# Gate and branch projections of a hybrid decoder layer with tokens instead of features on the output partitions

## The chip, the cores and the metric

The kernel runs on one core of one Trainium2 chip. The metric is the time of one execution on the device in microseconds (us). A profile is one further execution, taken by the hardware profiler; TensorE's rows stand under PE (products) and PEld (loads of the left operand), VectorE is DVE, ScalarE is ACT, GpSimd is POOL, and SP is SyncE, which here only issues DMAs.

## The reference

One layer with 256 tokens, model width 2048 and float32 throughout. The input is normalised and projected by `w_in` (2048 x 12288). Its columns feed three branches of width 1024 (a gMLP, an S5 state-space mixer, stick-breaking attention) and three gates of width 2048. The part that matters:

```python
h = rmsnorm(x, norm1_g[l])
proj = h @ w_in[l]
...
gates = jax.nn.sigmoid(proj[..., o_c:].reshape(bsz, seq, N_BRANCHES, D_MODEL) + b_gate[l])
...
ys = jnp.stack([y_a, y_b, y_c], axis=2)
br = jnp.einsum('blnw,nwd->blnd', ys, w_branch[l])
merged = jnp.sum(gates * br, axis=2)
x = x + merged @ w_out[l]
h2 = rmsnorm(x, norm2_g[l])
x = x + jnp.square(jax.nn.relu(h2 @ w_mlp_in[l])) @ w_mlp_out[l]
```

A row's norm is a factor per token; the kernel projects the input times the norm's weight and multiplies by that factor when it takes the product out of PSUM.

## The kernel before

**Products in three passes.** Every float32 product is done in TensorE's faster float32r type: each operand is split into a high part that is exact in that type and the rest, low. A product is high by high, low by high and high by low, added up in PSUM. A class `Split` holds an activation with features on partitions, high and low.

**Units.** All large weights run past as 536 units of 256 rows by 512 columns (512 KB) in one order (`plan`). For a unit SyncE issues the load (`dma_to`, four buffers, five units ahead), ScalarE copies the high part (L198) and VectorE subtracts it for the low one (the rows `lo<-raw,hi`), three units ahead of the products (`conv_to`). A group is the 4 or 8 units of one block of 512 output columns.

**Two forms.** `run_T` (L254) holds 128 x 128 blocks of the weights and streams the 256 tokens past them: the output has features on partitions and tokens along a row, 24 products of 256 columns for a unit (L265, L266 high weights, L273 low weights). `run_N` (L281) holds 128 x 128 blocks of the activation and streams 512 weight columns: the output has tokens on partitions, 12 products of 512 columns for a unit (L294, L295, L297). Both take a PSUM tile per half of a group, and hand it to the group's function `ev` one unit after its last product. A function `later` puts work off by some units.

**Order of the groups.** The projections of S5, attention and gMLP; then for each of four column blocks d gate 2, branch 2, gate 0, branch 0; the four groups of gate 1; two groups of S5's own gate (glu); the four groups of branch 1; the output projection; the MLP. Before the change, all gates and branches use `run_T`; v, the gMLP's v half, the output projection and the second half of the MLP use `run_N`.

**Gates and branches.** `do_gate` multiplies each half of the product by the token factor, which stands along the row (`rb`), and ScalarE adds the bias, one number per partition from the table `colv`, in the sigmoid (L973, four instructions of 128 x 256 for a group). `do_branch` multiplies the gate by the branch's product and adds it to the merged sum; at branch 1 it splits the sum into `ms` at once, which already has features on partitions, as the output projection wants it.

**Side work.** The small work of S5, attention and gMLP is written as generators. After each unit `pump` runs them as long as VectorE's estimated time allows (2560 ns for a unit), up to their next `yield`; `yield BAR` waits for the next unit. Everything is issued in program order on TensorE, VectorE, ScalarE and SyncE, so each engine works through the units with the side work in between. S5's side work lies in the gate stretch; its small products `py` (L716) read rotated states that VectorE has made.

Of the kernel before, what the change touches and what calls it, by code (L numbers as in the profile page):

```python
# [36 lines left out]
# columns of the per-feature vectors  # L37
C_G1, C_G2, C_BG, C_GM, C_D, C_GLU = 0, 16, 32, 80, 88, 96
NCOLS = 104


class Split:
    """A transposed activation [features, tokens] as hi + lo, both exact in float32r."""
# [21 lines left out]
class Metered:  # L65
    """The vector engine, with the time of what has been issued to it (ns)"""
# [22 lines left out]
def hybrid_trunk(  # L89
# [9 lines left out]
    cols: bass.AP,  # L99
    final_g: bass.AP,  # L100
# [37 lines left out]
    # -------------------------------------------------------- weight stream  # L138
# [64 lines left out]
    # ------------------------------------------------------- side work pump  # L203
    BAR = "bar"
    tasks = []
    credit = [0.0]  # vector engine time left to side work
# [24 lines left out]
    # -------------------------------------------------------- matmul groups  # L231
    slot = [0]
    late = []  # evacuations, emitted one unit after the group's last product
# [20 lines left out]
    def run_T(us, src, evac, lead=3, mid=None, delay=1):  # L254
        """out[512 features, tokens]; evac(b, psum [P, 2, T]) for each 256 features"""
        ps = [ps_mm.tile([P, 2, T], F32, tag="mm", name=f"mm{us[0]}_{b}") for b in range(2)]
        nk = len(us)
        for i, u in enumerate(us):
            hi, lo = begin_unit(u, lead)
            for nb in range(4):  # L260
                po = ps[nb // 2][:, nb % 2, :]
                for k in range(2):
                    kt = 2 * i + k
                    wh = hi[:, k, nb * P:(nb + 1) * P]
                    PE.matmul(po, lhsT=wh, rhs=src.hi(kt), start=kt == 0 and nb % 2 == 0, stop=False)  # L265
                    PE.matmul(po, lhsT=wh, rhs=src.lo(kt), start=False, stop=False)  # L266
                if nb == 1 and mid is not None:
                    mid(i)
            for nb in range(4):
                po = ps[nb // 2][:, nb % 2, :]  # L270
                for k in range(2):
                    kt = 2 * i + k
                    PE.matmul(po, lhsT=lo[:, k, nb * P:(nb + 1) * P], rhs=src.hi(kt), start=False,  # L273
                              stop=kt == 2 * nk - 1 and nb % 2 == 1)
            if i == nk - 1:
                for b in range(2):
                    late.append((slot[0] + delay, lambda b=b: evac(b, ps[b])))
                flush()
            end_unit()

    def run_N(us, src, evac):  # L281
        """out[tokens, 512 columns]; evac(tt, psum [P, 512]) for each 128 tokens"""
        ps = [ps_mm.tile([P, 512], F32, tag="mm", name=f"mm{us[0]}_{tt}") for tt in range(NT)]
        nk = len(us)
        for i, u in enumerate(us):
            hi, lo = begin_unit(u, 3)
            for part in range(2):
                for tt in range(NT):
                    for k in range(2):
                        kt = 2 * i + k  # L290
                        xh = src.hi(kt)[:, tt * P:(tt + 1) * P]
                        xl = src.lo(kt)[:, tt * P:(tt + 1) * P]
                        if part == 0:
                            PE.matmul(ps[tt], lhsT=xh, rhs=hi[:, k, :], start=kt == 0, stop=False)  # L294
                            PE.matmul(ps[tt], lhsT=xl, rhs=hi[:, k, :], start=False, stop=False)  # L295
                        else:
                            PE.matmul(ps[tt], lhsT=xh, rhs=lo[:, k, :], start=False,  # L297
                                      stop=kt == 2 * nk - 1)
            if i == nk - 1:
                for tt in range(NT):  # L300
                    late.append((slot[0] + 1, lambda tt=tt: evac(tt, ps[tt])))
            end_unit()

    def run_last(us, src, evac):
        """out[tokens, 512 columns], the first 128 tokens ahead of the others"""
        w = []
        nk = len(us)
        for tt, c0, c1 in ((0, 0, 512), (1, 0, 256), (1, 256, 512)):
            ps = ps_mm.tile([P, 512], F32, tag="mm", name=f"mml{tt}_{c0}")
            po = ps[:, 0:c1 - c0]  # L310
            for kt in range(2 * nk):
                if kt % 2 == 0 and tt == 0:
                    w.append(begin_unit(us[kt // 2], 7))
                    slot[0] += 1
                hi, lo = (t[:, kt % 2, c0:c1] for t in w[kt // 2])
                xh = src.hi(kt)[:, tt * P:(tt + 1) * P]
                xl = src.lo(kt)[:, tt * P:(tt + 1) * P]
                PE.matmul(po, lhsT=xh, rhs=hi, start=kt == 0, stop=False)
                PE.matmul(po, lhsT=xh, rhs=lo, start=False, stop=False)
                PE.matmul(po, lhsT=xl, rhs=hi, start=False, stop=kt == 2 * nk - 1)  # L320
            evac(tt, c0, c1, po)

    # ------------------------------------------------------------- helpers
    def inv_rms(ss, n, name):
        """ss [P, tiles, parts] partial sums of squares -> [P, tiles] (mean + eps) ** -0.5"""
# [15 lines left out]
    def split2(dst, i, src):  # L341
        """src [P, 2, T]: feature tiles 2 i and 2 i + 1"""
# [4 lines left out]
    def transposes(chunk, half, name):  # L347
        """two feature tiles, each in its own bank"""
# [9 lines left out]
    def split_scaled(pts, dst, kt0, gcol):  # L358
        """transposed feature tiles, times the norm's weight"""
# [7 lines left out]
    # ------------------------------------------------- first loads, constants  # L367
# [30 lines left out]
    # ntri[s', s] = -1 where s' > s  # L398
# [4 lines left out]
    # the tensor engine's clock comes up while the first loads are under way  # L403
    pw = side("pwarm")
    wz = cst([P, P], "wz")
    V.memset(wz, 0.0)
    def warm(n):
        for i in range(n):
            PE.matmul(pw[:, 0:P], lhsT=wz, rhs=wz, start=True, stop=True)
# [3 lines left out]
    # --------------------------------------------------------------- norm 1  # L413
# [36 lines left out]
    # ------------------------------------------------------------------- S5  # L450
    s5x = [a4([P, 4, T], F32, f"s5x{i}") for i in range(2)]  # input, then y, then gelu(y)
# [5 lines left out]
    def s5_split_b():  # L457
        """hi and lo of the input matrices, to DRAM; they come back stacked"""
# [52 lines left out]
    def s5_prep():  # L511
# [25 lines left out]
        # k = (exp(lam dt) - 1) / lam  # L537
# [19 lines left out]
        # e1[j, b] = exp(i phi b), e16[j, a] = exp(16 i phi a); cs ends as exp(128 i phi)  # L557
# [33 lines left out]
    def s5_run():  # L591
# [5 lines left out]
        def stack(ch):  # L597
            """u and b of two 32-row blocks, stacked so that one pass is bh uh + bl uh + bh ul"""
# [29 lines left out]
        def make_ck(h):  # L628
# [10 lines left out]
            # minus the imaginary part  # L639
# [4 lines left out]
        def table_a(ch):  # L644
            """exp(i phi t), t < 128"""
# [23 lines left out]
        def table_b(ch):  # L669
            """t >= 128, the parts that go with the sine"""  # L670
# [17 lines left out]
        def rotate(cs, z, sign):  # L688
            """z *= exp(sign i phi t)"""
# [88 lines left out]
    # ------------------------------------------------------------ attention  # L778
# [3 lines left out]
    def attention(half):  # L782
        scale = 1.0 / math.sqrt(P)
        fl = "p e b t -> p (e b t)"
        for hb in (2 * half, 2 * half + 1):
# [11 lines left out]
            for e in range(2):  # L797
                S.activation(za[:, e].rearrange("p b t -> p (b t)"), pz[e][:, 0:T + P], AF.Copy, scale=scale)
                # keep t > s in the two blocks on the diagonal
# [43 lines left out]
    # ----------------------------------------------------------------- gMLP  # L843
# [11 lines left out]
    def gmlp():  # L855
        ws, bs = gm["ws"], gm["bs"]
        # keep s <= t
# [36 lines left out]
    # ------------------------------------------------------- group handlers  # L894
# [68 lines left out]
    def do_gate(n, d, us):  # L963
        def ev(b, ps):
            if b == 0:
                gate[n, d] = a4([P, 4, T], F32, f"gate{n}_{d}")
            gt = gate[n, d]
            V.tensor_mul(gt[:, 2 * b:2 * b + 2, :], ps, rb)

            def act():  # L970
                for nb in (2 * b, 2 * b + 1):
                    c = C_BG + 16 * n + 4 * d + nb
                    S.activation(gt[:, nb, :], gt[:, nb, :], AF.Sigmoid, bias=colv[:, c:c + 1])  # L973

            later(1 + b, act)

        run_T(us, xs, ev)

    def do_branch(n, d, us):
        if n != 1:  # L980
            drain({2: "att1", 0: "gmlp"}[n])
        def ev(b, ps):
            gt = gate[n, d]
            if n == 2:
                merged[d] = gt
            g = gt[:, 2 * b:2 * b + 2, :]
            m = merged[d][:, 2 * b:2 * b + 2, :]
# [3 lines left out]
            if n == 1:  # L991
                split2(ms, 2 * d + b, m)

        run_T(us, {2: yc, 0: ya, 1: yb}[n], ev)
# [84 lines left out]
    # ------------------------------------------------------------- the trunk  # L1079
# [44 lines left out]
def _tiles(w):  # L1124
    """[K, N] -> [N / 512, K / 256, 128, 2, 512]: one contiguous half megabyte per unit"""
# [8 lines left out]
def _layout(x, norm1_g, w_in, b_gate, gm_norm_g, gm_w_s, gm_b_s, s5_lambda_re, s5_lambda_im, s5_log_dt,  # L1134
# [10 lines left out]
    a["cols"] = np.concatenate([_cols(norm1_g[0]), _cols(norm2_g[0]), _cols(b_gate[0]), _cols(gm_norm_g[0]),  # L1145
                                _cols(s5_d[0]), _cols(s5_b_glu[0])], axis=1)
    a["final_g"] = final_g
# [37 lines left out]
```

## Time and profile before

| | us |
|---|---|
| median of 3 runs | 1581.82 |
| lowest and highest | 1581.37 and 1581.89 |
| profiled execution, span from its first to its last instruction | 1579.1 |
| TensorE busy in it | 1564.4 |
| VectorE busy | 1069.1 |
| ScalarE busy | 763.5 |

The profile gives no time around the span of its execution; the median of the runs stands 2.7 us above it. Products are pipelined, so that a single one's row (283 ns for 256 columns, 389 for 512) is longer than its share of the time: what a unit takes is read from the start of one unit to the start of the next. Idle time of an engine that nothing waits for costs nothing.

### The profile page before, as it was taken

What the parts mean: (1) busy time and instruction counts of PE and PEld (TensorE: products, weight loads), DVE (VectorE), ACT (ScalarE), POOL (GpSimd) and SP (SyncE); (2) the same over time, 40 slices, a digit from 0 to 9 for tenths busy, and PEclk for the clock granted to TensorE, in tenths of its full rate; (3) what the DMA queues carried; (4) which work ended last, traced back from release to release, by engine and by line L of the source; (5) the groups of instructions that cost most, each with busy time, mean ns of one, the idle gap of its engine ahead of it and who ended that gap; (6) DMA issues with size and microseconds to landing.
All of it is one profiled execution on the core that took longest, in us unless ns stands there. A gap on an engine that the chain in (4) does not pass through costs nothing.

```text
span 1579.1 us, 26929 instructions
## 1 busy us (share of the span) xinstructions
PE 1564.4 (99%) x11030; PEld 1467.4 (93%) x11030; DVE 1069.1 (68%) x1402; ACT 763.5 (48%) x954; POOL 71.2 (5%) x126
## 2 busy tenths in 40 slices
PE   9999999999999999999999999999999999999996
PEld 9999989999999999999889998899888998899986
DVE  6895889988989898967655555555545555554554
ACT  6436567545454555464444444444433444344442
POOL 0102121000011000000000000000000000000000
PEclk9999999999999999999999999999999999999998
DMA  7868666666666666555665566656666566666663
GB/s 269 249 202 233 189 196 188 187 182 184 193 194 183 186 200 187 161 175 194 220 214 185 170 193 197 191 179 193 187 191 194 177 187 193 193 174 196 214 190 106
DMA packets 95258, 303.84 MB, mean 192 GB/s; under 512 B 11040, under 2 KB 22816, under 8 KB 95136
## 3 DMA queue, kind: packets, MB, share of 16 engines
q1 hardware_dynamic: 79840, 285.25, 59.6%
q0 software_dynamic: 11904, 10.49, 3.4%
q10 hardware_dynamic: 3392, 6.40, 1.2%
q8 instruction: 86, 1.41, 0.4%
q14 instruction: 36, 0.29, 0.1%
HBM read 295.80 MB, written 6.29 MB: 191 GB/s over the span
## 4 chain that ended last, share of the span: by engine, by line
PE 97%; issue 1%; DVE 1%; DMA 1%; ACT 0%; POOLq 0%; POOL 0%; DVEq 0%; ACTq 0%
PE mm L265 21%; PE mm L266 21%; PE mm L273 21%; PE mm L294 11%; PE mm L295 11%; PE mm L297 11%; PE py L716 1%; PE pb L618 0%; DVE x L83 0%; DMA raw<-in_w_m 0%; PE pyc L834 0%; DVE lo L83 0%; PE pm L878 0%; PE zt L353 0%; PE xt L353 0%
## 5 line engine op out<-in xcount | busy, mean ns | idle before, releaser
L83 DVE TENSOR_TENSOR lo<-raw,hi 128x1024 fp32r<-128x1024 f32 (+1 forms) x537 | 652.9, 1222 | 433.4 <-ACT hi L198 432.8
L198 ACT CAST hi<-raw 128x1024 fp32r<-128x1024 f32 (+1 forms) x537 | 557.8, 1048 | 645.6 <-PE mm L266 357.6
L265 PE MATMUL mm<-xs,hi 128*128 128x256 f32 x1280 | 316.0, 284 | 0.6 <-ACT hi L198 0.5
L266 PE MATMUL mm<-xs,hi 128*128 128x256 f32 x1280 | 314.1, 283 | 0.0
L265 PE MATMUL mm<-xz,hi 128*128 128x256 f32 x1024 | 251.4, 283 | 0.0
L266 PE MATMUL mm<-xz,hi 128*128 128x256 f32 x1024 | 251.3, 283 | 0.0
L265 PEld LDWEIGHTS mm<-xs,hi 128*128 128x128 f32 x1280 | 245.4, 192 | 3.5 <-ACT bu L625 2.1
L266 PEld LDWEIGHTS mm<-xs,hi 128*128 128x128 f32 x1280 | 245.5, 192 | 0.0
L266 PEld LDWEIGHTS mm<-xz,hi 128*128 128x128 f32 x1024 | 196.6, 192 | 0.2
L265 PEld LDWEIGHTS mm<-xz,hi 128*128 128x128 f32 x1024 | 196.6, 192 | 0.2
L295 PE MATMUL mm<-hi,ff 128*128 128x512 f32 x480 | 186.8, 389 | 0.0
L294 PE MATMUL mm<-hi,ff 128*128 128x512 f32 x480 | 186.8, 389 | 0.0
L273 PE MATMUL mm<-xs,lo 128*128 128x256 f32 x1280 | 179.7, 283 | 0.0
L273 PEld LDWEIGHTS mm<-xs,lo 128*128 128x128 f32 x1280 | 165.1, 192 | 0.0
L273 PE MATMUL mm<-xz,lo 128*128 128x256 f32 x1024 | 143.7, 283 | 0.0
L273 PEld LDWEIGHTS mm<-xz,lo 128*128 128x128 f32 x1024 | 132.1, 192 | 0.0
L297 PE MATMUL mm<-lo,ff 128*128 128x512 f32 x480 | 128.3, 389 | 0.0
L297 PEld LDWEIGHTS mm<-lo,ff 128*128 128x128 f32 x480 | 90.1, 188 | 18.7
L295 PEld LDWEIGHTS mm<-hi,ff 128*128 128x128 f32 x480 | 90.1, 188 | 18.6
L294 PEld LDWEIGHTS mm<-hi,ff 128*128 128x128 f32 x480 | 90.1, 188 | 18.6
L83 DVE TENSOR_TENSOR rt<-bu,cs 128x1024 f32<-128x1024 f32 x64 | 76.4, 1219 | 0.2
L294 PE MATMUL mm<-hi,xs 128*128 128x512 f32 x128 | 50.5, 394 | 0.0
(241 smaller groups left out, 1732.9 us busy)
## 6 DMA issues: line engine op xcount, KB each, us to landing
raw<-in_w_m SPq DMA_DIRECT2D x256, 512.0 KB, 4.3
raw<-in_w_in SPq DMA_DIRECT2D x191, 512.0 KB, 4.1
raw<-in_w_br SPq DMA_DIRECT2D x48, 512.0 KB, 4.2
raw<-in_w_out SPq DMA_DIRECT2D x32, 512.0 KB, 4.4
raw<-in_w_glu SPq DMA_DIRECT2D x8, 512.0 KB, 4.2
su<-ud POOLq DMA_DIRECT2D x48, 64.0 KB, 5.1
bs<-bd POOLq DMA_DIRECT2D x48, 64.0 KB, 4.8
x<-in_x ACTq DMA_DIRECT2D x4, 512.0 KB, 5.4
```

The costliest lines, as they stand in the source:

```text
L83: return fn(*a, **kw)
L198: S.copy(hi[:, k, :], raw[:, k, :])
L265: PE.matmul(po, lhsT=wh, rhs=src.hi(kt), start=kt == 0 and nb % 2 == 0, stop=False)
L266: PE.matmul(po, lhsT=wh, rhs=src.lo(kt), start=False, stop=False)
L273: PE.matmul(po, lhsT=lo[:, k, nb * P:(nb + 1) * P], rhs=src.hi(kt), start=False, stop=kt == 2 * nk - 1 and nb % 2 == 1)
L294: PE.matmul(ps[tt], lhsT=xh, rhs=hi[:, k, :], start=kt == 0, stop=False)
L295: PE.matmul(ps[tt], lhsT=xl, rhs=hi[:, k, :], start=False, stop=False)
L297: PE.matmul(ps[tt], lhsT=xh, rhs=lo[:, k, :], start=False, stop=kt == 2 * nk - 1)
L716: PE.matmul(py[h][32 * i:32 * i + 32, :T], lhsT=cks[h][:, ri, i, :], rhs=s[i // 2][:, ri, i % 2, :], start=ri == 0, stop=ri == 1, tile_pos ...
```

## The change

Gate and branch groups use `run_N`. The bias then lies along the row: each gate group loads its 512 numbers spread over all partitions, three units after its start, into one buffer, and VectorE does scale and bias in one instruction. The merged sum has tokens on partitions, so a generator `merged_T` turns it for the output projection, two column tiles of 128 at a time, and splits it. The gate bias leaves the table `colv`, and the first warm-up products read `ones` in place of a zeroed tile. Comments are left out of the file, which moves its line numbers.

```diff
+    b_gate: bass.AP,
...
-    wz = cst([P, P], "wz")
-    V.memset(wz, 0.0)
     def warm(n):
         for i in range(n):
-            PE.matmul(pw[:, 0:P], lhsT=wz, rhs=wz, start=True, stop=True)
+            PE.matmul(pw[:, 0:P], lhsT=ones, rhs=ones, start=True, stop=True)
...
     def do_gate(n, d, us):
-        def ev(b, ps):
-            if b == 0:
-                gate[n, d] = a4([P, 4, T], F32, f"gate{n}_{d}")
-            gt = gate[n, d]
-            V.tensor_mul(gt[:, 2 * b:2 * b + 2, :], ps, rb)
-
-            def act():
-                for nb in (2 * b, 2 * b + 1):
-                    c = C_BG + 16 * n + 4 * d + nb
-                    S.activation(gt[:, nb, :], gt[:, nb, :], AF.Sigmoid, bias=colv[:, c:c + 1])
-
-            later(1 + b, act)
-
-        run_T(us, xs, ev)
+        gb = []
+
+        def bias():
+            gb.append(s5w.tile([P, 512], F32, tag="gb", name=f"gb{n}_{d}", bufs=1))
+            S.dma_start(gb[0], b_gate[n, d * 512:(d + 1) * 512].partition_broadcast(P))
+
+        later(3, bias)
+
+        def ev(tt, ps):
+            if tt == 0:
+                gate[n, d] = a4([P, NT, 512], F32, f"gate{n}_{d}")
+            gt = gate[n, d][:, tt, :]
+            V.scalar_tensor_tensor(out=gt, in0=ps, scalar=r1[0][:, tt:tt + 1], in1=gb[0],
+                                   op0=ALU.mult, op1=ALU.add)
+            later(1 + tt, lambda: S.activation(gt, gt, AF.Sigmoid))
+
+        run_N(us, xs, ev)
+
+    def merged_T(d):
+
+        for half in range(2):
+            yield BAR
+            pts = transposes(merged[d], half, f"mt{d}_{half}")
+            yield BAR
+            for j, pt in enumerate(pts):
+                split1(ms, 4 * d + 2 * half + j, pt[:, :T])
+            yield 900
 
     def do_branch(n, d, us):
...
-        def ev(b, ps):
-            gt = gate[n, d]
+
+        def ev(tt, ps):
             if n == 2:
-                merged[d] = gt
-            g = gt[:, 2 * b:2 * b + 2, :]
-            m = merged[d][:, 2 * b:2 * b + 2, :]
+                merged[d] = gate[n, d]
+            g = gate[n, d][:, tt, :]
+            m = merged[d][:, tt, :]
             V.tensor_mul(g, g, ps)
             if n != 2:
                 V.tensor_add(m, m, g)
-            if n == 1:
-                split2(ms, 2 * d + b, m)
-
-        run_T(us, {2: yc, 0: ya, 1: yb}[n], ev)
+            if n == 1 and tt == 1:
+                spawn(f"mt{d}", merged_T(d))
+
+        run_N(us, {2: yc, 0: ya, 1: yb}[n], ev)
```

TensorE's row, in a gate group (unit 108, the first of gate 0's first group). In the names, `mm108_0` and `mm108_1` are the two PSUM tiles of the group that begins with unit 108, `hi108` and `lo108` the unit's weights, `xs0` the normalised input's first 256 features. Before, the last products of the unit and the small products of S5 behind it (`pb6`):

```order
L265 MATMUL mm108_1_3999<-xs0_145,hi108_3895 128x256
L266 MATMUL mm108_1_3999<-xs0_145,hi108_3895 128x256
L273 MATMUL mm108_0_3998<-xs0_145,lo108_3896 128x256 x4
L273 MATMUL mm108_1_3999<-xs0_145,lo108_3896 128x256 x4
L618 MATMUL pb6_0_4042<-su6_3416,bs6_3415 128x256 x2
L618 MATMUL pb6_1_4045<-su6_3416,bs6_3415 128x256 x2
L265 MATMUL mm108_0_3998<-xs1_176,hi109_3931 128x256
L266 MATMUL mm108_0_3998<-xs1_176,hi109_3931 128x256
```

Now, the same place:

```order
L296 MATMUL mm108_1_3853<-hi108_3787,xs0_143 128x512
L297 MATMUL mm108_1_3853<-hi108_3787,xs0_143 128x512
L299 MATMUL mm108_0_3852<-lo108_3788,xs0_143 128x512 x2
L299 MATMUL mm108_1_3853<-lo108_3788,xs0_143 128x512 x2
L618 MATMUL pb6_0_3884<-su6_3414,bs6_3413 128x256 x2
L618 MATMUL pb6_1_3887<-su6_3414,bs6_3413 128x256 x2
L296 MATMUL mm108_0_3852<-hi109_3810,xs1_174 128x512
L297 MATMUL mm108_0_3852<-hi109_3810,xs1_174 128x512
```

The products with the low weights, two rows of four with 256 columns, have become two rows of two with 512; those with the high weights go from 16 to 8 in the same way (the last two of the unit stand here). S5's small products keep their place behind the unit.

TensorE's row at the second unit of the output projection (units 248 to 255; `ms1`, `ms2` are 256 features each of the split merged sum). Before:

```order
L294 MATMUL mm248_1_9049<-hi249_8988,ms1_8665 128x512
L295 MATMUL mm248_1_9049<-hi249_8988,ms1_8665 128x512
L297 MATMUL mm248_0_9048<-lo249_8989,ms1_8665 128x512 x2
L297 MATMUL mm248_1_9049<-lo249_8989,ms1_8665 128x512 x2
L294 MATMUL mm248_0_9048<-hi250_9018,ms2_8792 128x512
L295 MATMUL mm248_0_9048<-hi250_9018,ms2_8792 128x512
```

Now:

```order
L296 MATMUL mm248_1_7362<-hi249_7314,ms1_7183 128x512
L297 MATMUL mm248_1_7362<-hi249_7314,ms1_7183 128x512
L299 MATMUL mm248_0_7361<-lo249_7315,ms1_7183 128x512 x2
L299 MATMUL mm248_1_7362<-lo249_7315,ms1_7183 128x512 x2
L355 MATMUL mt3_0_0_7408<-ident_111,gate2_3_5573 128x128 x2
L355 MATMUL mt3_0_1_7411<-ident_111,gate2_3_5573 128x128 x2
L296 MATMUL mm248_0_7361<-hi250_7337,ms2_7230 128x512
L297 MATMUL mm248_0_7361<-hi250_7337,ms2_7230 128x512
```

Four transposes of the last column block's sum (`mt3_0`) stand between the second and the third unit of the output projection; the other four (`mt3_1`) follow after the fourth.

ScalarE's row in the second group of gate 2 (units 120 to 127; `gb2_1` is its bias, `gate2_1` its gate, `td7` and `bu8` belong to S5). Before, around the sigmoids:

```order
L198 CAST hi128_4638<-raw128_4563 128x1024
L198 CAST hi129_4670<-raw129_4605 128x1024
L198 CAST hi130_4707<-raw130_4636 128x1024
L198 CAST hi131_4743<-raw131_4668 128x1024
L198 CAST hi132_4776<-raw132_4705 128x1024
L973 ACT_TABLE_LOAD
L973 ACTIVATE gate2_1_4747<-gate2_1_4747,colv_105 128x256 x2
L609 DMA ct4_4814<-in_s5_c 128x256
L198 CAST hi133_4824<-raw133_4741 128x1024
L973 ACTIVATE gate2_1_4747<-gate2_1_4747,colv_105 128x256 x2
```

Now, around the load of the bias and the sigmoids:

```order
L199 CAST hi125_4217<-raw125_4175 128x1024
L199 CAST hi126_4239<-raw126_4197 128x1024
L968 DMA gb2_1_4243<-in_b_gate 128x512
L676 ACTIVATE td7_4261<-cs7_4168,s5_cs_721 128x128 x4
L199 CAST hi127_4271<-raw127_4215 128x1024
L199 CAST hi128_4290<-raw128_4237 128x1024
L199 CAST hi129_4310<-raw129_4269 128x1024
L199 CAST hi130_4335<-raw130_4288 128x1024
L199 CAST hi131_4359<-raw131_4308 128x1024
L199 CAST hi132_4380<-raw132_4333 128x1024
L978 ACT_TABLE_LOAD
L978 ACTIVATE gate2_1_4363<-gate2_1_4363 128x512
```

The load of the bias stands between the weight copies of units 126 and 127, and the sigmoids of the group behind the copy of unit 132 as before, two instead of four.

## Rows read from the trace of the kernel before

**Rows 1.** The page: span, busy time of the engines, chain that ended last.
```profile
span 1579.1 us, 26929 instructions
...
PE 1564.4 (99%) x11030; PEld 1467.4 (93%) x11030; DVE 1069.1 (68%) x1402; ACT 763.5 (48%) x954; POOL 71.2 (5%) x126
...
PE 97%; issue 1%; DVE 1%; DMA 1%; ACT 0%; POOLq 0%; POOL 0%; DVEq 0%; ACTq 0%
```

**Rows 2.** Windows: v projection; gate stretch; last branch; output projection. Busy us per engine.
```profile
core 0: us, PE busy (x) PEld busy (x) DVE busy (x) ACT busy (x) POOL busy (x), PEclk, DMA share, GB/s
...
102.23:124.02 21.79, 21.79 (x98) 18.04 (x97) 17.38 (x37) 9.34 (x10) 1.53 (x2) 1.00 0.77 215
...
305.55:689.61 384.06, 384.06 (x3242) 379.75 (x3241) 341.30 (x470) 198.53 (x265) 25.11 (x48) 1.00 0.65 186
...
712.65:758.73 46.08, 46.08 (x386) 46.08 (x385) 33.55 (x38) 22.56 (x29) 0.00 (x0) 1.00 0.57 182
...
758.73:848.50 89.77, 89.77 (x410) 74.27 (x409) 51.30 (x56) 43.17 (x59) 0.00 (x0) 1.00 0.67 216
```

**Rows 3.** Timeline of TensorE, two run_T units: start us, length us, instruction.
```profile
393.79 1.12 PE L273 MATMUL mm<-xs,lo 128*128 128x256 f32 x8
...
396.67 1.12 PE L273 MATMUL mm<-xs,lo 128*128 128x256 f32 x8
```

**Rows 4.** Timeline of TensorE, two run_N units of the v projection.
```profile
106.80 1.07 PE L297 MATMUL mm<-lo,xs 128*128 128x512 f32 x4
...
109.52 1.07 PE L297 MATMUL mm<-lo,xs 128*128 128x512 f32 x4
```

**Rows 5.** Timeline of TensorE in the output projection, with its transposes.
```profile
785.05 1.07 PE L297 MATMUL mm<-lo,ms 128*128 128x512 f32 x4
...
785.97 0.60 PE L353 MATMUL zt<-ident,x 128*128 128x128 f32 x4
...
791.90 0.60 PE L353 MATMUL zt<-ident,x 128*128 128x128 f32 x4
...
796.90 1.07 PE L297 MATMUL mm<-lo,ms 128*128 128x512 f32 x4
```

**Rows 6.** Groups by shape, VectorE: count, busy us, mean ns of one, idle before.
```profile
L83 DVE TENSOR_TENSOR gate<-mm,rbc 128x512 f32<-128x512 f32 x24 | 15.4, 683 | 0.0
...
L83 DVE SCALAR_TENSOR_TENSOR x<-mm,rsq,x 128x512 f32<-128x512 f32 x30 | 21.3, 744 | 0.0
...
L83 DVE TENSOR_TENSOR ms<-gate,ms 128x512 fp32r<-128x512 f32 x8 | 5.5, 692 | 5.5 <-ACT ms L344 5.5
...
L83 DVE TENSOR_TENSOR yc<-pyc,yc 128x256 fp32r<-128x256 f32 x8 | 3.1, 416 | 0.0
```

**Rows 7.** Windows: a stretch with VectorE full, and a light unit after it.
```profile
597.49:620.53 23.04, 23.04 (x195) 23.04 (x194) 22.94 (x32) 9.59 (x13) 0.00 (x0) 1.00 0.58 174
...
623.41:627.85 4.44, 4.44 (x46) 3.72 (x44) 2.43 (x2) 3.29 (x7) 0.00 (x0) 1.00 0.80 205
```

**Rows 8.** Waits of SyncE's queue in 297 to 689 us: total, times, longest.
```profile
SPq L179 <- DVE lo L83: 336.8, 129, 5.8
```

**Rows 9.** Timeline around the last state products: VectorE, then TensorE.
```profile
672.30 1.29 DVE L83 TENSOR_TENSOR bu<-rt,rt 128x512 f32<-128x512 f32 x2
...
677.00 1.07 PE L716 MATMUL py<-bu,ck 128*32 128x256 f32 x16
```

**Rows 10.** Timeline at a branch group's end: TensorE, then VectorE.
```profile
746.25 1.12 PE L273 MATMUL mm<-yb,lo 128*128 128x256 f32 x8
...
747.58 1.22 DVE L83 TENSOR_TENSOR lo<-raw,hi 128x1024 fp32r<-128x1024 f32 x1 [1.14 <-ACT hi L198]
...
748.72 0.68 DVE L83 TENSOR_TENSOR gate<-gate,mm 128x512 f32<-128x512 f32 x1
```

**Rows 11.** The page: DMA issues, KB each, median us to landing.
```profile
fg<-in_final_g ACTq DMA_DIRECT2D x2, 512.0 KB, 6.7
```

**Rows 12.** Timeline of the start: the memsets of both tiles.
```profile
0.79 0.20 POOL L392 MEMSET ones<- 128x128 f32 x1 [0.29 <-POOLq L1176]
...
0.92 0.17 DVE L83 MEMSET wz<- 128x128 f32 x1
```

More of the change, by code (lines that the diff above doesn't have):

```diff
@@ L35 @@
 MAGIC = 12582912.0
-C_G1, C_G2, C_BG, C_GM, C_D, C_GLU = 0, 16, 32, 80, 88, 96
-NCOLS = 104
+C_G1, C_G2, C_GM, C_D, C_GLU = 0, 16, 32, 40, 48
+NCOLS = 56
 class Split:
@@ L290, in run_N @@
                         kt = 2 * i + k
+                        assert src.t[kt // 2] is not None
                         xh = src.hi(kt)[:, tt * P:(tt + 1) * P]
@@ L1144, in _layout @@
     a["w_m2"] = _tiles(w_mlp_out[0])
-    a["cols"] = np.concatenate([_cols(norm1_g[0]), _cols(norm2_g[0]), _cols(b_gate[0]), _cols(gm_norm_g[0]),
+    a["cols"] = np.concatenate([_cols(norm1_g[0]), _cols(norm2_g[0]), _cols(gm_norm_g[0]),
                                 _cols(s5_d[0]), _cols(s5_b_glu[0])], axis=1)
+    a["b_gate"] = b_gate[0]
     a["final_g"] = final_g
```

## The prediction

> **What bounds the kernel now.** I read the page's busy shares and its chain first. They show TensorE busy for 99% of a span of 1579.1 us, and 97% of the chain that ended last is TensorE's own instructions, one behind the other [rows 1]. So no stall is there to be removed: the time can only fall if the products themselves take less, or rise if something new makes TensorE wait. The second view was the windows by stage: in the gate stretch, the branch stretch and the output projection TensorE is busy all the time at a granted clock of 1.00, the 2.4 GHz level [rows 2]. The third was the timeline, for the length of one weight unit (256 x 512 weights) in either form. With features on the output partitions (run_T) the last block of a unit starts at 393.79 us and that of the next at 396.67: 2.88 us for 24 products of 256 columns, 0.120 us each [rows 3]. With tokens on the output partitions (run_N) it is 106.80 to 109.52: 2.72 us for 12 products of 512 columns, 0.227 us each [rows 4]. Both do the same multiplications; two products of 256 cost 0.240, one of 512 costs 0.227. The run_N rows are from the v projection, which has the same left operand (the normalised input) and the same weight array as the gates will have.
>
> **What the change takes away.** It moves 12 gate groups of 8 units and 12 branch groups of 4 units from run_T to run_N: 144 units, each 2.88 - 2.72 = 0.16 us shorter, 23.0 us in all. TensorE is the path in the whole stretch, so all of this counts. 128 of the units lie in the gate stretch of 384.06 us [rows 2]; at 2.88 us they fill 368.6 of it, and the other 15.4 are the small products of the state-space branch and the gMLP, which stay. The stretch should come to 384.1 - 20.5 = 363.6 us. The other 16 units are the stretch of the last branch, 46.08 us now.
>
> **What it adds on TensorE.** The merged sum now has tokens on partitions, so each of its four column groups is turned by 8 transposes, 32 in all. The output projection does the same to its own result already: from 785.05 to 796.90 us lie four run_N units and 8 transposes, 11.85 us, and four units are 10.88 [rows 5]. So 8 transposes cost 0.97 us on the path, and four groups 3.9 us. The Trainium skill, TensorE: Matmul & The Clock Gate, section on the PE-mode transpose, gives about 275 ns for one transpose in a kernel. A single transpose lasts that long in this trace too, but four of them take 0.60 us from first start to last end [rows 5], since they overlap. By the page's figure taken singly, 32 would cost 8.8 us and the time would be 1567.6 us; the sum here goes by the rows.
>
> **What it adds elsewhere, at no cost.** VectorE: the 24 gate evacuations become scale-and-add from PSUM; the nearest row with such an operation of that size is 744 ns against 683 [rows 6], 1.5 us in all. The 8 split subtractions of 692 ns become 16 of 256 columns, where the nearest row has 416 [rows 6]: 1.2 us more. Its multiplications and additions in the branches keep their size and number. ScalarE gets 24 sigmoids of 512 in place of 48 of 256 and stays half idle (198.53 us busy of 384.06 [rows 2]). Whether VectorE still hides this is the one real question, because in the gate stretch it is busy for 341.30 us of 384.06 [rows 2], and would be for 342.8 of 363.6, 94%. It does not run out on the mean. In places it does: over eight units from 597.49 us it is busy for 22.94 of 23.04 us [rows 7]. Eight run_N units last 21.76, so there it falls behind by some 1.3 us, the dearer evacuations included. Soon after comes a unit with small products of S5 behind it, 4.44 us with 2.43 us of work for VectorE [rows 7], which gives it back. What queues behind it: the low halves of the weights, converted three units (8 us) ahead; the weight loads, which SyncE issues only after such a conversion (129 waits in this stretch [rows 8]) into four buffers; and TensorE's small products that read the rotated states. The last are the tightest: at 677.00 us they start 3.4 us after VectorE finished their input at 673.59 [rows 9]. A lag of 1.3 us fits. I take no loss here, and keep a loss of some us in the range.
>
> The transposes wait for the last addition of their group. A branch group's products end at 747.2 us now; VectorE then has a conversion, and multiplies and adds from 748.72 on [rows 10], four operations of 0.69 us at most, done by about 751.4. The transposes stand two units, 5.44 us, behind the group's end, at 752.6: 1.2 us to spare. Of the last group, the second half is turned after four units of the output projection and split by ScalarE and VectorE during the next one or two; it is first read in the eighth.
>
> The bias is now loaded by ScalarE's queue, 256 KB spread over all partitions, three units into a gate group and wanted five units (13.6 us) later. The nearest row, a spread load of 512 KB on the same queue, lands after 6.7 us [rows 11]. The load waits for the readers of the bias before, which were due three units earlier. Nothing waits. At the start the warm-up products read a tile of ones that GpSimd has at 0.99 us in place of one that VectorE has at 1.09 [rows 12]: no difference.
>
> **Sum.** 1579.1 - 23.0 + 3.9 = 1560.0 us of span. The median of the runs, 1581.82 us, stands 2.7 above the profiled span; with that kept, 1562.7 us, 1.2% less than before.
>
> **Rivals.**
> First, VectorE sets the pace. If each stretch in which it is full keeps its length, most of the 20.5 us in the gate stretch stays unearned. Half of it lost is about 1573 us; all of it lost, with the 1.5 us of dearer evacuations, is 1562.7 + 20.5 + 1.5 = 1584.7, just within 0.2% of before. For it speaks the 89% share, against it the 43 us in which VectorE now idles in this stretch and the 3.4 us at the tightest reader [rows 2, 9].
> Second, the 0.16 us does not belong to the form. A product's fixed part is 256 columns at 2.4 GHz, 0.1067 us, taken from 0.120, and 512 columns, 0.2133, taken from 0.2267: 0.013 us either way. If that part were a fifth of this, the unit would gain 0.03 us, 144 units 4.3, and the transposes would eat it: 1581.4 us, no change. The Trainium skill, on the same page under the back-to-back issue gap, puts the fixed part at 2.5 ns, which is this case; the trace has 13 ns in both forms [rows 3, 4] and so speaks against it.
> Third, on the other side: the bias load is late. Each gate group's evacuation waits for its own load, everything on VectorE behind it stands, and TensorE follows once the 3.4 us at the state products are used up. It decides from a landing of 13.6 + 3.4 = 17.0 us; at 20 us it costs 12 x 3 = 36 us, 1598.7 us, slower. The row says 6.7 us for twice the bytes.
>
> **How the numbers follow.** The forecast, with at most some us lost: 0.83. VectorE's pace with a part of the gain lost: 0.10, of which 0.02 is no change. The fixed part: 0.03. The late load: 0.03. What none of these names: 0.01, slower. A difference of 0.2% (3.2 us) is about what a measurement of this kernel can tell from none. So faster 0.91, same 0.05, slower 0.04. The range: below, the transposes at nothing give 1558.8; above, 5 us lost to VectorE give 1568. That leaves out 2 in 10 at most.
>
> **What would show it.** Right: gate and branch units of 2.72 us, the gate stretch at about 364 us with VectorE at 94% of it, the last branch stretch at about 46.4 us (16 x 2.72 and three groups of transposes), no wait of TensorE for VectorE over 1 us, the bias landing within 7 us. Wrong: gate units of 2.8 us and more, or idle time of TensorE ahead of the state products or the transposes.

## The result and the profile after

The changed kernel takes 1563.81 us, the median of four runs (1562.95 to 1565.1). The kernel before took 1581.66 beside it (1581.37 to 1581.89). The ratio is 0.9888, with a 95% interval of 0.9876 to 0.9900: 1.1% less time, where 1562.7 us and 1.2% were forecast.

The head of the page of the kernel after and its chain of work answer to [rows 1]:

```profile
span 1562.8 us, 23528 instructions
...
PE 1548.3 (99%) x9334; PEld 1382.7 (88%) x9334; DVE 1069.4 (68%) x1409; ACT 759.5 (49%) x938; POOL 71.2 (5%) x126
...
PE 97%; issue 1%; DVE 1%; DMA 1%; ACT 0%; POOLq 0%; POOL 0%; DVEq 0%; ACTq 0%
```

TensorE is as busy as before, 99%, with 1,696 instructions fewer (1,728 products less, 32 transposes more). The time was not won from a stall: the same work takes less time in fewer products. VectorE's busy time is the same to 0.3 us.

The windows by stage of the kernel after (columns as in [rows 2]): the gate stretch, its part up to the third gate, the last branch, the output projection.

```profile
core 0: us, PE busy (x) PEld busy (x) DVE busy (x) ACT busy (x) POOL busy (x), PEclk, DMA share, GB/s
307.73:671.98 364.25, 364.25 (x1707) 299.42 (x1705) 341.13 (x470) 193.08 (x243) 25.08 (x48) 1.00 0.65 204
307.73:581.92 274.19, 274.19 (x1287) 226.05 (x1285) 258.54 (x363) 145.37 (x185) 25.08 (x48) 1.00 0.66 205
695.01:741.34 46.33, 46.33 (x218) 38.31 (x217) 32.99 (x42) 23.39 (x33) 0.00 (x0) 1.00 0.59 198
741.34:832.38 91.04, 91.04 (x419) 75.31 (x418) 52.01 (x60) 44.03 (x62) 0.00 (x0) 1.00 0.61 204
```

The gate stretch has gone from 384.06 to 364.25 us, the last branch from 46.08 to 46.33, and the output projection takes 91.04 us where the same 32 units took 89.97 before (in [rows 2] it starts at 758.73, and the next unit after it at 848.70). VectorE's share of the gate stretch has risen from 89% to 94% (341.13 of 364.25), with TensorE still busy throughout.

The timeline of TensorE in the kernel after: two gate units, the answer to [rows 3], and then the transposes of the merged sum among output projection units, the answer to [rows 5]. Columns: start us, length us, instruction.

```profile
349.05 1.07 PE L299 MATMUL mm<-lo,xs 128*128 128x512 f32 x4
351.77 1.07 PE L299 MATMUL mm<-lo,xs 128*128 128x512 f32 x4
...
746.01 1.07 PE L299 MATMUL mm<-lo,ms 128*128 128x512 f32 x4
746.92 0.60 PE L355 MATMUL mt<-ident,gate 128*128 128x128 f32 x4
749.21 1.07 PE L299 MATMUL mm<-lo,ms 128*128 128x512 f32 x4
751.92 1.07 PE L299 MATMUL mm<-lo,ms 128*128 128x512 f32 x4
```

A gate unit is 2.72 us long (351.77 less 349.05), as the v projection's was [rows 4]. A unit with four transposes is 3.20 (749.21 less 746.01), 0.48 more, so eight cost 0.97 as in [rows 5]. The transposes that start at 746.92 us read a sum that VectorE had finished at 745.24, 1.7 us ahead, where 1.2 were forecast. The row of its last addition:

```profile
744.55 0.69 DVE L83 TENSOR_TENSOR gate<-gate,gate 128x512 f32<-128x512 f32 x1
```

TensorE's waits in the whole kernel after (engine and line, what it waited for, total us, times, longest):

```profile
PE pwarm L409 <- POOL ones L394: 1.0, 1, 1.0
PE pyc L834 <- ACT le L826: 0.8, 1, 0.8
PE xt L355 <- DMA x<-in_x: 0.7, 1, 0.7
```

None of the three lies in the stretches that were changed, and none names VectorE. The last state products, the tightest place in [rows 9], look like this after (timeline, VectorE and then TensorE):

```profile
656.52 1.28 DVE L83 TENSOR_TENSOR bu<-rt,rt 128x512 f32<-128x512 f32 x2
...
659.92 1.07 PE L716 MATMUL py<-bu,ck 128*32 128x256 f32 x16
```

Their input is finished 2.12 us ahead of them (659.92 less 657.80), where it was 3.4 before: VectorE is 1.3 us later here, the lag that the forecast allowed for. The new operations on VectorE by shape, the answer to [rows 6], and the bias load in the list of DMA issues, the answer to [rows 11]:

```profile
L83 DVE SCALAR_TENSOR_TENSOR gate<-mm,r_r,gb 128x512 f32<-128x512 f32 x24 | 16.9, 746 | 0.0
...
L83 DVE TENSOR_TENSOR ms<-mt,ms 128x256 fp32r<-128x256 f32 x16 | 6.0, 417 | 0.0
```

```profile
gb<-in_b_gate ACTq DMA_DIRECT2D x12, 256.0 KB, 4.2
```

They took 746 and 417 ns where 744 and 416 were forecast. The bias lands after 4.2 us in the median and after 6.7 at the latest, and 13.6 us were there for it.

**Where the forecast's span is missed.** The span was to be 1560.0 us and is 1562.8. Of the 2.8 us, 2.2 lie ahead of anything that was changed: the gate stretch begins at 307.73 us, not at 305.55. Most of that is in the first 12 us. TensorE's timeline there in this profile (transposes of x, warm-up products, and 256-column products of the first unit):

```profile
4.72 1.09 PE L355 MATMUL xt<-ident,x 128*128 128x128 f32 x4 [0.75 <-DMA x<-in_x]
5.60 1.49 PE L409 MATMUL pwarm<-ones 128*128 128x128 f32 x6
...
7.78 0.41 PE L267 MATMUL mm<-xs,hi 128*128 128x256 f32 x1
7.99 0.41 PE L266 MATMUL mm<-xs,hi 128*128 128x256 f32 x1
...
10.51 0.28 PE L267 MATMUL mm<-xs,hi 128*128 128x256 f32 x1
10.63 0.28 PE L266 MATMUL mm<-xs,hi 128*128 128x256 f32 x1
```

Up to 9.9 us a product starts 0.21 us after the one before it, and from 10.3 us on 0.12 us after it. These are the two levels of the clock, 1.2 and 2.4 GHz; the trace's record of the granted clock begins, at full, at 10.18 us. In the profile of the kernel before it begins at 4.38 us, and the same rows read:

```profile
4.40 0.63 PE L353 MATMUL xt<-ident,x 128*128 128x128 f32 x4 [0.33 <-DMA x<-in_x]
4.86 0.83 PE L409 MATMUL pwarm<-wz 128*128 128x128 f32 x6
```

TensorE ran twelve warm-up instructions ahead of these in both (a product of plain float32 operands stands as two, so these are the program's six). In the later case it then stood idle for 0.75 us, waiting for the first load of x, and in the earlier one for 0.33.

### The profile page after: what moved, and what is told of

Its sections match the earlier page's. It is cut to its first block, busy times and chain, and to the rows that moved or that the text cites. A ratio compares the mean times of both kernels' runs of the same rounds, so it can differ in the third digit from the quotient of the medians.

```text
span 1562.8 us, 23528 instructions
## 1 busy us (share of the span) xinstructions
PE 1548.3 (99%) x9334; PEld 1382.7 (88%) x9334; DVE 1069.4 (68%) x1409; ACT 759.5 (49%) x938; POOL 71.2 (5%) x126
## 4 chain that ended last, share of the span: by engine, by line
PE 97%; issue 1%; DVE 1%; DMA 1%; ACT 0%; POOLq 0%; POOL 0%; DVEq 0%; ACTq 0%
PE mm L296 19%; PE mm L297 19%; PE mm L299 19%; PE mm L266 12%; PE mm L267 12%; PE mm L274 12%; PE py L716 1%; PE pb L618 0%; DVE x L83 0%; PE xt L355 0%; DMA raw<-in_w_m 0%; DMA x<-in_x 0%; PE pyc L834 0%; PE pc L817 0%; DVE lo L83 0%
## 5 line engine op out<-in xcount | busy, mean ns | idle before, releaser
L296 PE MATMUL mm<-hi,xs 128*128 128x512 f32 x512 | 200.8, 392 | 0.0
L297 PE MATMUL mm<-hi,xs 128*128 128x512 f32 x512 | 199.5, 390 | 0.0
L299 PE MATMUL mm<-lo,xs 128*128 128x512 f32 x512 | 137.0, 389 | 0.0
L266 PE MATMUL mm<-xs,hi 128*128 128x256 f32 x512 | 127.8, 287 | 0.0
L267 PE MATMUL mm<-xs,hi 128*128 128x256 f32 x512 | 126.5, 284 | 0.0
L296 PEld LDWEIGHTS mm<-hi,xs 128*128 128x128 f32 x512 | 96.1, 188 | 21.8 <-ACT bu L625 2.1
L299 PEld LDWEIGHTS mm<-lo,xs 128*128 128x128 f32 x512 | 96.1, 188 | 20.2
L297 PEld LDWEIGHTS mm<-hi,xs 128*128 128x128 f32 x512 | 96.2, 188 | 19.4
```

The costliest lines, as they stand in the source:

```text
L299: PE.matmul(ps[tt], lhsT=xh, rhs=lo[:, k, :], start=False, stop=kt == 2 * nk - 1)
```

## The experiments

All ran beside the kernel before. Three more questions were open: whether the late clock belongs to the change, whether the 0.16 us belongs to the form or to the number of columns, and how much room VectorE has left.

**The changed kernel a second time** (no edit).

> The changed kernel once more, five rounds. Theory: its work past the first 16 us is fixed, and what varies is when TensorE's clock rises at the start (10.2 us in its first profile, 4.4 us in that of the kernel before; 1.9 us of the span). Then its runs fall between 1562 and 1565.5 us and its profile spans 1560.9 us where the clock rises before the first unit and 1562.8 where it rises after 10 us. Rival: the 2 us are lost for good by something in the change. Then every profile has the late rise and no run is below 1562.9.

It took 1562.99 us (1562.87 to 1563.64), ratio 0.9882 (0.9868 to 0.9895), with a span of 1561.2. The same place in its timeline:

```profile
4.85 0.83 PE L409 MATMUL pwarm<-ones 128*128 128x128 f32 x6
...
7.17 0.39 PE L266 MATMUL mm<-xs,hi 128*128 128x256 f32 x1 [0.43 <-ACT hi L199]
7.39 0.28 PE L267 MATMUL mm<-xs,hi 128*128 128x256 f32 x1
```

Here the same six rows took 0.83 us and the clock's record begins at 4.20 us, in the same program. The late clock differs between executions, then, and is no part of the change. The kernel before varies as much: its 15 runs beside this one lie between 1580.28 and 1584.74 us. The first unit waits 0.43 us for ScalarE's copy of its weights, which makes 0.4 of the 0.6 us by which the gate stretch, at 306.14 us, begins later than before the change. The stretch is again 364.25 us long.

**Zeroes for the warm-up of the changed kernel.** The warm-up reads a tile of zeroes that VectorE sets, as before the change.

```diff
+    wz = a4([P, P], F32, "wz")
+    V.memset(wz, 0.0)
...
-            PE.matmul(pw[:, 0:P], lhsT=ones, rhs=ones, start=True, stop=True)
+            PE.matmul(pw[:, 0:P], lhsT=wz, rhs=wz, start=True, stop=True)
```

> The changed kernel with its warm-up products on a zeroed tile again, as before (the tile comes from the pool of activations). Theory of chance: the operand's value has no part in when the clock rises; median within 1 us of the changed kernel, the same spread of about 2 us. Rival, that the ones delay the clock: median 1561.9 (1.9 us below the changed kernel), spread 0.5 us as the kernel before has.

1564.05 us (1563.29 to 1564.76), ratio 0.9889 (0.9874 to 0.9904); the clock's record begins at 6.84 us. Zeroes do not bring the clock up sooner, and the median is 0.2 us from the changed kernel's first, not 1.9 below it.

**Ones for the warm-up of the kernel before**, the same edit the other way.

```diff
-    wz = cst([P, P], "wz")
-    V.memset(wz, 0.0)
...
-            PE.matmul(pw[:, 0:P], lhsT=wz, rhs=wz, start=True, stop=True)
+            PE.matmul(pw[:, 0:P], lhsT=ones, rhs=ones, start=True, stop=True)
```

> The kernel before with warm-up products on the tile of ones, nothing else changed. Theory of chance: 1581.7 us, as before. Rival, that the ones delay the clock: 1583.6 us (1.9 us more) in most runs, or a spread of 2 us.

1581.42 us (1580.23 to 1584.2), ratio 0.9999 (0.9990 to 1.0007); the record begins at 5.74 us. The spread of 4 us meets the rival's second sign to the letter, but the kernel before spreads by 4.5 us beside it. Nothing shows that this part of the change is worth anything either way.

**More warm-up products in the changed kernel.**

```diff
-NWARM = 6
+NWARM = 8
```

> The changed kernel with 8 warm-up products ahead of the first transposes in place of 6. They end at about 4.5 us instead of 4.0, so that TensorE hardly idles until the input lands at 4.4 to 4.7. Theory that the clock's rise hangs on what TensorE did just before: an early rise in all runs, 1562 us with a spread under 1 us. Rival, chance of the moment alone: median and spread as the changed kernel (1563.8, 2 us).

1563.00 us (1562.68 to 1563.05), ratio 0.9881 (0.9867 to 0.9894); the record begins at 5.63 us. Its median is that of the second run of the changed kernel. Its runs lie within 0.4 us, as the first theory asked, but not at 1562, and the changed kernel's second four lie within 0.8 us with no edit at all, so this run does not decide. What sets the moment at which the clock rises stays open: it was 4.20 to 10.18 us over the five profiles of this group and of the changed kernel, with no order by operand.

**The new form with products of 256 columns.** Gates and branches keep the tokens on the output partitions, but each product of 512 columns is cut in two.

```diff
+                        if cut:
+                            for x_ in ((xh, xl) if part == 0 else (xh,)):
+                                for c in range(2):
+                                    cc = slice(256 * c, 256 * c + 256)
+                                    PE.matmul(ps[tt][:, cc], lhsT=x_, rhs=(lo if part else hi)[:, k, cc],
...
-        run_N(us, xs, ev)
+        run_N(us, xs, ev, cut=True)
```

> The changed kernel, but each product of the gates and branches is cut into two of 256 columns, with the same left operand loaded twice: 24 products for a unit again, in the new layout. Theory, the fixed 0.013 us belongs to each product whatever the operands: units of 2.88 us, the 23.0 us come back, 1586.8 us (gate stretch 384.7 us). Rival, the layout itself is faster (evacuation, banks, operands): units stay at 2.72 us, 1563.8 us.

1585.1 us (1583.28 to 1586.13), ratio 1.0021 (1.0011 to 1.0031): slower than the kernel before, and 1.7 us under the 1586.8 expected. Windows of its gate stretch and last branch:

```profile
304.47:688.53 384.06, 384.06 (x3242) 379.75 (x3241) 342.43 (x470) 192.78 (x243) 25.10 (x48) 1.00 0.68 194
711.58:760.17 48.59, 48.59 (x411) 48.59 (x409) 33.03 (x43) 23.30 (x33) 0.00 (x0) 1.00 0.63 193
```

The gate stretch is 384.06 us to the hundredth, as in [rows 2], in the other layout. So the gain hangs on the number of products, not on which side the tokens are. Against the changed kernel the two windows are 22.1 us longer (19.8 and 2.3). The transposes are still paid, which makes the last branch 48.59 us where it was 46.08. One thing stays open: the edit doubles the loads of the left operand with the products, and PEld is busy for 379.75 of 384.06 us in either layout [rows 2], so this run does not tell a product's own fixed part from that of its load.

**Half of the change.** Column blocks 0 and 1 in the new form, 2 and 3 in the old one (the bias as a column, products in run_T).

```diff
+        if d >= 2:
+            def ev_t(b, ps):
...
+            run_T(us, xs, ev_t)
+            return
```

> Column blocks 0 and 1 of gates and branches in the new form, 2 and 3 in the old one. Theory, the gain is 0.16 us for each moved unit less 0.97 us for each transposed block: 72 units and 2 blocks, 11.5 - 1.9 = 9.6 us below the kernel before, 1572.1 us (up to 1.9 more with a late rise of the clock). Rival, a fixed part is gained or lost once (a change of form, the first evacuations): the half gains clearly more or less than half of 17.8 us, by 2 us or more.

1571.66 us (1571.62 to 1572.18), ratio 0.9934 (0.9919 to 0.9948). The kernel before took 1581.74 us beside it, so half of the units give 10.1 of the 17.9 us (9.6 expected). The gain is counted in units, then, and no single place of the kernel gives it.

**One more operation on VectorE per unit.** In the 96 gate and branch units up to the third gate, a memset of 128 x 128 is added at each unit's start. It writes a tile that nobody reads by then.

```diff
+            for _ in range(1 if load else 0):
+                nc.vector.memset(nones, -1.0)
```

> The changed kernel with one more memset of 128 x 128 on VectorE (about 0.13 us of its time) in each of the 96 units of gates and branches 2 and 0, some 12 us. VectorE is busy for 258.5 of the 274.2 us of this stretch. Theory, VectorE is hidden until it is full: 271 of 274, time within 2 us of the changed kernel. Rival, VectorE already sets the pace in the full stretches: 8 to 12 us more. Rival, VectorE has no part at all: no change here and none with three memsets.

1562.95 us (1562.78 to 1563.26), ratio 0.9878 (0.9863 to 0.9893). The window of that stretch:

```profile
306.51:580.70 274.19, 274.19 (x1287) 226.05 (x1286) 265.11 (x459) 144.87 (x185) 25.11 (x48) 1.00 0.68 204
```

VectorE is busy 6.6 us longer than in the same window of the changed kernel, and the stretch is 274.19 us in both. VectorE is not the bound. A single memset holds it for 0.08 us, as its timeline shows:

```profile
404.20 0.17 DVE L289 MEMSET nones<- 128x128 f32 x1
404.28 1.17 DVE L83 TENSOR_TENSOR lo<-raw,hi 128x1024 fp32r<-128x1024 f32 x1
```

**Three such operations per unit.**

```diff
+            for _ in range(3 if load else 0):
+                nc.vector.memset(nones, -1.0)
```

> The same with three memsets in each of the 96 units, some 37 us more on VectorE: 295 us of work in 274. Theory, hidden until full: TensorE waits for the difference, 15 to 25 us more than the changed kernel, and the idle time of TensorE shows it ahead of the products on the weights or of the state products. Rival, it sets the pace already: 35 us and more. Rival, no part: no change.

1599.58 us (1599.42 to 1599.88), ratio 1.0109 (1.0094 to 1.0125): 36.6 us more than the changed kernel's second run, where 15 to 25 were expected. By the number alone this is the rival that VectorE sets the pace already (35 us and more). The windows of the same stretch and of the rest of the gate stretch; TensorE's longest waits; and VectorE's timeline around one trio:

```profile
305.94:614.66 308.72, 287.07 (x1287) 226.14 (x1285) 289.08 (x631) 137.95 (x181) 25.08 (x48) 0.99 0.59 178
614.66:706.92 92.26, 91.15 (x423) 73.07 (x422) 88.94 (x129) 49.40 (x63) 0.00 (x0) 1.00 0.63 207
```

```profile
PE mm L301 <- DVE lo L83: 18.0, 24, 1.9
PE py L718 <- DVE bu L83: 4.6, 3, 1.9
```

```profile
390.93 0.68 DVE L289 MEMSET nones<- 128x128 f32 x3
391.53 1.19 DVE L83 TENSOR_TENSOR lo<-raw,hi 128x1024 fp32r<-128x1024 f32 x1
```

Now TensorE waits for VectorE, at the two places that the prediction named: the low halves of the weights, and the rotated states. What was mis-sized is the load. A trio holds VectorE for 0.60 us (391.53 less 390.93): each memset starts 0.26 us after the one before it (the trio's row is 0.68 long and a single one's 0.17, which leaves 0.51 for two), and only the last lets the next instruction start 0.08 us later. 96 trios are 57.6 us, where the expectation had 37. VectorE's waits in the first window add up to 1.0 us, so it is full there. The two windows together are 400.98 us, 36.7 more than the changed kernel's 364.25. So 20.9 of the 57.6 us were hidden, about 0.22 for each of the 96 units, and that is near the 23.1 us in which VectorE idles in the changed kernel's gate stretch (364.25 less 341.13). The rival falls with this and with the single memset, which cost nothing.

TensorE's waits are 22.6 of the 36.6 us. Most of the rest stands as busy time (287.07 us in the first window where it was 274.19). Twice in it, at 404 and at 582 us, the granted clock fell to the 1.2 GHz level soon after a wait of 1.85 us. TensorE's timeline at the first of them, where products then start 0.43 us apart in place of 0.23:

```profile
403.08 1.22 PE L301 MATMUL mm<-lo,xs 128*128 128x512 f32 x4 [1.85 <-DVE lo L83]
...
404.52 0.63 PE L299 MATMUL mm<-hi,yc 128*128 128x512 f32 x1
404.95 0.63 PE L298 MATMUL mm<-hi,yc 128*128 128x512 f32 x1
```

**The step that the runs point to.** The MLP's first product is the last long stretch of run_T, and VectorE is half idle there. It is put into run_N too: relu and square with tokens on the partitions, then transposes.

```diff
+        def ff_T():
+            for half in range(2):
+                yield BAR
+                pts = transposes(t[0], half, f"ft{q}_{i}_{half}")
+                yield BAR
+                for j, pt in enumerate(pts):
+                    split1(ffs[q], 4 * i + 2 * half + j, pt[:, :T])
...
-        run_T(us, xs2, ev)
+        run_N(us, xs2, ev)
```

> Changed kernel, with the MLP's first product also computed with tokens on the output partitions (run_N): relu and square on [tokens, features], then 8 transposes and a split for each of the 16 column groups. Theory (0.16 us for each unit of 512-column products, 0.97 us for 8 transposes, VectorE hidden): 128 units x 0.16 = 20.5 us less, 16 x 0.97 = 15.5 us more, so 5 us less: 1558 us where the changed kernel has 1563; units of 2.72 us in the MLP's first halves. Rival (the chain of relu, square, transposes and split is late for the second product, which reads a group's features 6 units later): TensorE waits there, and the time is 1563 us or more.

1558.12 us (1557.73 to 1559.36), ratio 0.9849 (0.9836 to 0.9863): 4.9 us less than the changed kernel's 1562.99, where 5 were expected, and the fastest version of all. TensorE waits for nothing in the MLP. Three column groups of this kernel in the windows, and then the same three of the changed kernel's second run:

```profile
853.74:921.92 68.18, 68.18 (x314) 56.40 (x312) 37.01 (x42) 32.12 (x43) 0.00 (x0) 1.00 0.59 186
```

```profile
854.69:923.81 69.12, 69.12 (x579) 69.12 (x577) 36.89 (x36) 31.21 (x37) 0.00 (x0) 1.00 0.56 183
```

A group of 8 units takes 22.73 us where it took 23.04: 8 x 0.16 less 0.97 is 0.31, and 16 groups make 5.0. This group pays its own transposes, so three quarters of the gain go to them. The 12 gate groups need no transposes, and the 12 branch groups only four sets.

## Why the prediction was right

**The unit.** 2.72 us after, 0.16 less than before, as taken from [rows 3, 4]. In the gate stretch 117 of 128 units are shorter by 0.15 or 0.16; the other 11, at the stretch's start and right behind units with the gMLP's and the states' small products, gain 0.07 to 0.14. That is why the stretch gained 19.8 us and not 20.5, and is 0.65 longer than forecast; six units behind the states' products, at 0.07 to 0.09, make 0.45 of it.

**The transposes.** 0.97 us per eight, 3.9 in all, as read from [rows 5]. The last branch came to 46.33 us (46.4 forecast), and the output projection to 1.07 more with the fourth set and a trail of 0.1. The longer figure that the Trainium skill gives for one transpose (TensorE: Matmul & The Clock Gate, PE-mode transpose) would have made 8.8 us; four in a stream cost 0.48 us on TensorE's path here.

**VectorE.** 94% busy in the gate stretch (341.13 us, where 342.8 were forecast), 1.3 us later at the tightest reader, no wait of TensorE for it: as forecast, and the two runs with added load show that the cover is real and how far it goes. That was the first rival. Its trigger exists, but some 0.2 us per unit beyond this kernel.

**The fixed part of a product.** The second rival, a fixed part of a fifth of 0.013 us, falls: cutting the products in two gave back the whole 0.16 us per unit, 0.013 us for each of 12 added products. The Trainium skill (TensorE: Matmul & The Clock Gate, back-to-back issue gap) gives 2.5 ns for an isolated product, and says that this figure leaves out the load of the left operand. Here each product has such a load, and the trace has 13 ns. The load alone does not bring it, though. The attention's products of plain float32 operands in the kernel after (start, length, instruction; the rows write f32 for float32r as well, and the program's types tell the two apart):

```profile
224.74 0.59 PE L817 MATMUL pc<-sp,ntri 128*128 128x256 f32 x2
225.17 0.38 PE L819 MATMUL pc<-sp,nones 128*128 128x128 f32 x2
225.39 0.39 PE L820 MATMUL pc<-sp,ntri 128*128 128x128 f32 x2
225.61 0.60 PE L817 MATMUL pc<-sp,ntri 128*128 128x256 f32 x2
```

The two with 256 columns take 0.43 us, 0.215 each, and the four with 128 take 0.44, 0.11 each. Half the columns take about half the time, which leaves some 0.005 us for a fixed part (twice 0.11 less 0.215), under half of 0.013. The 0.013 us is shown for the float32r products alone, and why they have it stays open.

**The bias.** Landing in 4.2 us, not the 17.0 from which the third rival would decide. Neither VectorE nor TensorE waits for it; one wait of ScalarE, of 1.7 us, is put down to it, and nothing on TensorE's path follows from that.

**What was wrong.** Two small terms, outside the change, in opposite directions. "No difference" at the start was sized from one profile. The start differs by 1.6 us between two profiles of the same kernel (gate stretch from 307.73 or 306.14 us), and a further 0.2 to 0.3 lies in one attention unit with small products (4.55 us before, 4.77 and 4.84 after) whose cause no run isolated. And the 2.7 us kept above the span was too much: the profiled execution of the changed kernel took 1564.47 us, 1.7 above its span, and the other nine profiled here stand 1.7 to 1.8 above theirs. The execution profiled before the change has no time of its own on record. The kernel before's runs beside the experiments stand 1.8 to 1.9 above their spans; by that it took some 1580.9, about 0.9 less than the median against which it was set. The 1.0 us too much and the 2.8 too little make 1.8, of which the median shows 1.1. So it is in part luck that the forecast lies as near as 1.1 us: without the first error it would have been 2.1 us off.

Over the whole profile the sum closes: 19.8 less in the gate stretch, 0.25 more in the last branch, 1.07 more in the output projection and 2.2 more ahead of them make 16.3, and the spans differ by 16.3.

## What to carry to other kernels

Where TensorE is busy throughout, count products and not operations: of two forms with the same work the one with fewer and wider products wins by the fixed part of each, here 0.013 us for float32r products that each load their left operand. Measure that part for the type at hand, and set the transposes that a layout needs against it per group. Before such a change, work out the share of the next engine in the shortened stretch and its margin at the tightest reader, since what follows depends on that cover. And set a profile's span against the time of that very execution; a median of other runs can be a microsecond off, and one profile does not size a start that varies.

## What the runs showed that was not expected

The full clock came between 4.20 and 10.18 us after the start, in two executions of the same program; the later one began its gate stretch 1.6 us later. A memset right behind another of the same tile starts 0.26 us after it, while other work behind a memset starts after 0.08, so an engine can be full while its busy time reads 289.08 of 308.72 us; whether the common tile is the cause was not tried. Products of plain float32 operands show no fixed part of 0.013 us, though each loads its left operand too.
